# Other places for the transposes of the first and the last experts, for the base rows and for the last additions

## The chip, the cores and the metric

The kernel runs on one core of a Trainium2 chip. The metric is the device time of one execution in microseconds (us). The engines are TensorE (PE, matmuls; PEld its weight loads), VectorE (DVE), ScalarE (ACT), GpSimd (POOL) and SyncE (SP), which issues most DMAs.

## What is computed

One block of a language model, for 512 tokens of width 1024 in fp32: an embedding layer norm, a gated delta-rule branch and a differential-attention branch that are mixed, a layer norm, and then a hierarchical mixture of 16 experts of width 256, two for each token, plus a gated embedding term and the last layer norm. The part that matters here:

```python
def hierarchical_moe(h, w_rg, b_rg, w_re, b_re, w_gate, w_up, w_down):
    ...
    hid = jax.nn.silu(jnp.einsum('bsd,edf->bsef', h, w_gate)) * jnp.einsum('bsd,edf->bsef', h, w_up)
    return jnp.einsum('bsef,efd->bsd', hid * combine[..., None].astype(h.dtype), w_down)
...
    ffn = hierarchical_moe(h, w_router_group[i], b_router_group[i], w_router_expert[i],
                           b_router_expert[i], w_exp_gate[i], w_exp_up[i], w_exp_down[i])
    ple = jax.nn.sigmoid(h @ w_ple_gate[i] + b_ple_gate[i]) * (p[i] @ w_ple_proj[i])
    h = layer_norm(alpha * h + ffn + ple, ln2_g[i], ln2_b[i])
```

## The kernel before

The first 498 us (branches, first norm, router, gated embedding term) are not touched. What follows is the loop over the 16 experts and then `finish`.

Every large product is made of three fp32r matmuls: both operands are split into a high part (a copy on ACT, rounded to fp32r) and a low part (the difference, on DVE). `mm3` issues high by high, high by low and low by high. For weights, `split_to` makes such a split in pieces of [128 x 1024], one ACT copy (L260) and one DVE subtraction (L261) each: sE are the gate and up weights of an expert (four pieces), sD the down weights (two pieces). `load_to` issues the weight loads on SP (L241); a load waits for the landing of the third one before it. `weights` keeps 9 loads and 4 splits ahead of their use.

Expert e goes through these steps:

- `gather` (L1171): an indirect DMA on POOL fetches the rows of up to 128 tokens into xr, one of three buffers, three experts ahead.
- `turn_x` (L1178): 8 transposes on PE (psx) and, for each half, the high part on ACT (L1185) and the low part on DVE (L1187). The result xT is "x(e)" in this text.
- `up` (L1190): 24 matmuls (pup), then the gate: a tanh on ACT (L1194) and two DVE instructions (L1195, L1196); its result is the tile eth.
- `turn_h` (L1199): 2 transposes (psf), a copy on ACT (L1205), the low part on DVE (L1207): hT, "h(e)".
- `down` (L1210): two halves of 6 matmuls (pdn), each scaled into y by ACT (L1220); then an indirect DMA on POOL, the scatter (L1223), writes y to its rows of `planes` in DRAM. `planes` holds two summands for each token. Each scatter waits for the landing of the one before.

The experts are staggered: the list of PE is up(e), x(e+1), down(e-1), h(e). The last two experts, `LAST`, are not scattered. Their scaled results stay in SBUF (`ykeep`, L1217 and L1218), and `finish` adds them by a matmul with a one-hot matrix `to_row`, which POOL makes in 8 instructions (L1288), listed behind the scatter of expert 13.

At e = 13 (IFE) the base rows (`load_base`, acc to the tiles at, 4 loads of 512 KB, L1272) are loaded. Behind the scatter of expert 13 `load_planes` fetches the four planes (pl, 1 MB each, L1277), and `add_planes` adds them to the base rows on DVE (L1283), two additions a tile.

`finish` does the last adding, norm and store for four tiles of 128 tokens: `spread` (PE, plast, L1378), `add_last` (DVE L1385, ACT square sq L1388), `dev` (DVE L1391 and a power on POOL, L204), `norm` (DVE L1395), `turn` (PE transposes into banks pzt, L1404), and `leave`, eight copies with scale and offset for each pair of tiles, on ACT (L1417) or DVE (L1419) as a string of letters says, with two stores on SP (L1422) for each pair.

The program order of each engine is what a scheduler makes of the order in which the instructions are written; PE, DVE and ACT then run their lists strictly in that order. Single PSUM banks come from two pools, `bank` (tag T) and `gbank` (tag G).

Of the kernel before, what the change touches and what calls it, by code (L numbers as in the profile page):

```python
# [19 lines left out]
D = 1024  # L20
NT = 4
# [50 lines left out]
def block_kernel(ctx, tc, x, pT, wA, wB, wO, wM, wPG, wPP, wE, wD, cols, rows, consts, out):  # L72
# [155 lines left out]
    raw, parts = {}, {}  # L228
# [22 lines left out]
    def split_to(n, lo_eng=DVE):  # L251

        while nsplit[0] < min(n, 2 * len(stream)):
            i, j = divmod(nsplit[0], 2)
            k, _, _, shp = stream[i]
            load_to(i + 1)
            n2, w = shp[0] // 2, shp[1]
            r = raw[i][:, j * n2:(j + 1) * n2, :]
            hl = big([2, n2, w], F32R, name="s" + k)
            ACT.activation(hl[:, 0], r, AF.Copy)  # L260
            lo_eng.tensor_tensor(hl[:, 1], r, hl[:, 0].bitcast(F32), op=OP.subtract)  # L261
            parts[i, j] = hl
            if j:
                raw.pop(i)
            nsplit[0] += 1
# [924 lines left out]
    def up(xT, gu, mmul, th=None):  # L1190
        ps = gbank("pup")
        steps(mmul(ps, 8, lambda k: ((xT[:, 0, k, :], xT[:, 1, k, :]), gu(k))))
        th = mid([512], name="eth") if th is None else th
        ACT.activation(th[:, :256], ps[:, :256], AF.Tanh, scale=0.5)  # L1194
        DVE.scalar_tensor_tensor(th[:, :256], th[:, :256], 1.0, ps[:, :256], op0=OP.add, op1=OP.mult)  # L1195
        DVE.tensor_tensor(th[:, 256:], th[:, :256], ps[:, 256:], op=OP.mult)  # L1196
        return th
# [12 lines left out]
    def down(hT, dw, wcol, idxs, mmul, keep=None, y=None):  # L1210
        y = half_slot("y") if keep is None and y is None else y
        for nh in range(2):
            ps = gbank("pdn")
            sl = slice(nh * 512, (nh + 1) * 512)
            steps(mmul(ps, 2, lambda f: ((hT[:, 0, f, :], hT[:, 1, f, :]), dw(f, sl))))
            if keep is not None:
                ACT.activation(keep[:, 0, sl], ps, AF.Copy, scale=wcol)  # L1217
                DVE.scalar_tensor_tensor(keep[:, 1, sl], ps, wcol, keep[:, 0, sl].bitcast(F32), op0=OP.mult, op1=OP.subtract)  # L1218
                continue
            ACT.activation(y[:, sl], ps, AF.Copy, scale=wcol)  # L1220
# [47 lines left out]
    at, pl = [], []  # L1268
# [5 lines left out]
    def load_planes():  # L1274
        pl[:] = [big([2, 1024], name="pl") for _ in range(NT)]
        for t in range(NT):
# [13 lines left out]
    def keep_expert(e):  # L1290
        ykeep[e] = big([2, 1024], F32R, name="ykeep")
        down(hTs.pop(e), weights("D", e), ecol("w", e), None, mm3, keep=ykeep[e])
# [8 lines left out]
    def beyond():  # L1301
        top = nc.values_load(RT["n"][:1, 16:17], min_val=0, max_val=S)
        with tc.If(top > 128):
# [28 lines left out]
            load_planes()  # L1332
            add_planes(*range(NT))
            finish(False)

    for e in range(NE):
        if e + AHEAD < NE:
            rows_of[e + AHEAD] = gather(ecol("s", e + AHEAD), e + AHEAD)
        if e == IFE:
            at = [big([2, 1024], name="at") for _ in range(2)]  # L1340
            load_base()
        if e in LAST:
            find_rows(e)
# [12 lines left out]
        if e + 1 == LAST[0]:  # L1356
            xTs[e + 1] = turn_x(rows_of.pop(e + 1), True)
            finish_expert(e)
            load_planes()
        if e == NE - 1:  # L1360
            with behind(DVE):
                add_planes(1)
# [3 lines left out]
    def finish(add=True):  # L1366
# [57 lines left out]
        with strict(DVE, ACT, PE):  # L1424
# [25 lines left out]
            leave(1, b1, "AVAVAVAV", 2)  # L1450
# [96 lines left out]
```

## Time and profile before

| what | value |
|---|---|
| median of 3 runs | 698.07 us (697.55 to 698.27) |
| the profiled execution | 699.76 us |
| its span, first to last instruction | 698.0 us |
| mean granted TensorE clock | 0.972 |
| TensorE busy | 661.2 us, 95% |
| VectorE busy | 501.3 us, 72% |
| ScalarE busy | 371.8 us, 53% |

The share of an engine is a mean over stages: TensorE is busy for almost the whole span, and the stages in which it isn't are found in the windows and timelines below. A number in brackets in a timeline is the time that the engine stood idle before an instruction, and what it then waited for last. All rows are of one profiled execution, times in us from the start of its span.

### The profile page before, as it was taken

How to read it: one execution, taken by the hardware profiler on the slowest of the kernel's cores; microseconds unless marked ns; L12 is line 12 of the kernel's file. 1: busy time of each engine (PE TensorE's matmuls, PEld its weight loads, DVE VectorE, ACT ScalarE, POOL GpSimd, SP SyncE). 2: the span in 40 equal slices, each digit the busy share in tenths (PEclk: the TensorE clock that was granted, in tenths of full speed). 3: DMA queues.
4: the chain of work that ended last, by engine and by line, in shares of the span. 5: the costliest groups of instructions: out<-in, count | busy, mean ns of one | idle time of the engine just before them, and what ended most of it. 6: DMA issues, size and time to landing. Idle time of an engine off the chain costs nothing. (4 is left out here: it accounts for less than half of the span.)

```text
span 698.0 us, 9556 instructions
## 1 busy us (share of the span) xinstructions
PE 661.2 (95%) x3504; PEld 551.6 (79%) x3505; DVE 501.3 (72%) x921; ACT 371.8 (53%) x695; POOL 98.4 (14%) x110
## 2 busy tenths in 40 slices
PE   8889999999999999999999999999989999997883
PEld 5788888888878878888788888899868888885652
DVE  4864786995358675865525366879689999998593
ACT  6633563472357564754514232134468899978333
POOL 2400030100011212200000010201111222211410
PEclk9899999999999999999999999999989999999995
DMA  8993004213104310312513543575699999994603
GB/s 331 372 418 129 0 13 147 113 61 86 67 1 144 121 62 1 120 61 83 219 61 121 203 161 123 201 297 185 220 375 366 393 361 359 374 360 197 253 0 124
DMA packets 31764, 127.17 MB, mean 182 GB/s; under 512 B 9585, under 2 KB 11249, under 8 KB 20576
## 3 DMA queue, kind: packets, MB, share of 16 engines
q1 hardware_dynamic: 27392, 118.73, 45.8%
q0 software_dynamic: 4320, 7.77, 3.1%
q8 instruction: 29, 0.48, 0.3%
q14 instruction: 23, 0.19, 0.1%
HBM read 111.91 MB, written 22.54 MB: 193 GB/s over the span
## 5 line engine op out<-in xcount | busy, mean ns | idle before, releaser
L283 PE MATMUL pg<-hTh,sA 128*128 128x512 f32 x320 | 129.7, 405 | 0.0
L285 PE MATMUL pg<-hTh,sA 128*128 128x512 f32 x320 | 126.8, 396 | 0.0
L284 PE MATMUL pg<-hTl,sA 128*128 128x512 f32 x320 | 126.7, 396 | 0.0
L261 DVE TENSOR_TENSOR sE<-wE,sE 128x1024 fp32r<-128x1024 f32 x64 | 75.1, 1218 | 0.3 <-ACT sE L260 0.3
L285 PEld LDWEIGHTS pg<-hTh,sA 128*128 128x128 f32 x320 | 60.2, 188 | 13.1
L283 PEld LDWEIGHTS pg<-hTh,sA 128*128 128x128 f32 x320 | 60.3, 188 | 11.6
L284 PEld LDWEIGHTS pg<-hTl,sA 128*128 128x128 f32 x320 | 60.3, 189 | 11.2
L260 ACT ACTIVATE sE<-wE 128x1024 fp32r<-128x1024 f32 x64 | 64.2, 1068 | 0.5 <-PE pg L285 0.4
L260 ACT ACTIVATE sA<-wA 128x1024 fp32r<-128x1024 f32 x40 | 41.4, 1054 | 37.3 <-PE pg L285 25.7
L261 DVE TENSOR_TENSOR sA<-wA,sA 128x1024 fp32r<-128x1024 f32 x40 | 48.5, 1218 | 15.3 <-ACT sA L260 15.3
L283 PE MATMUL pup<-sE,xT 128*128 128x512 f32 x128 | 53.4, 417 | 1.5 <-ACT xT L1185 1.4
L285 PE MATMUL pup<-sE,xT 128*128 128x512 f32 x128 | 52.3, 409 | 2.1 <-DVE xT L1187 2.1
L284 PE MATMUL pup<-sE,xT 128*128 128x512 f32 x128 | 52.1, 407 | 0.0
L261 DVE TENSOR_TENSOR sD<-wD,sD 128x1024 fp32r<-128x1024 f32 x32 | 37.8, 1221 | 4.8 <-ACT sD L260 4.6
L284 PE MATMUL pg<-sPG,H1H 128*128 128x262 f32 (+1 forms) x128 | 36.6, 286 | 0.0
L283 PE MATMUL pg<-sPG,H1H 128*128 128x262 f32 (+1 forms) x128 | 36.5, 286 | 0.0
L285 PE MATMUL pg<-sPG,H1L 128*128 128x262 f32 (+1 forms) x128 | 36.4, 285 | 0.0
L864 ACT ACTIVATE tt<-tt,mn 128x128 f32<-128x128 f32 (+3 forms) x32 | 17.8, 557 | 29.1 <-DVE mn L862 29.0
L260 ACT ACTIVATE sD<-wD 128x1024 fp32r<-128x1024 f32 x32 | 32.4, 1079 | 0.0
L285 PEld LDWEIGHTS pup<-sE,xT 128*128 128x128 f32 x128 | 25.1, 196 | 8.6 <-DVE xT L1187 2.9
L1174 POOL DMA_INDIRECT xr<-h1d,ts x16 | 17.8, 1113 | 98.5 <-PE psx L1183 66.0
L283 PEld LDWEIGHTS pup<-sE,xT 128*128 128x128 f32 x128 | 25.1, 196 | 7.5 <-ACT xT L1185 2.5
(360 smaller groups left out, 1553.1 us busy)
## 6 DMA issues: line engine op xcount, KB each, us to landing
wE<-wE SPq DMA_DIRECT2D x32, 1024.0 KB, 9.3
wA<-wA SPq DMA_DIRECT2D x20, 1024.0 KB, 5.2
wD<-wD SPq DMA_DIRECT2D x16, 1024.0 KB, 10.0
wPG<-wPG SPq DMA_DIRECT2D x4, 1048.0 KB, 8.8
planes<-nil SPq DMA_DIRECT2D x4, 1024.0 KB, 12.4
wO<-wO SPq DMA_DIRECT2D x4, 1024.0 KB, 4.8
wM<-wM SPq DMA_DIRECT2D x4, 1024.0 KB, 4.7
pl<-planes SPq DMA_DIRECT2D x4, 1024.0 KB, 10.9
```

Of the source, the lines that this page charges most:

```text
L260: ACT.activation(hl[:, 0], r, AF.Copy)
L261: lo_eng.tensor_tensor(hl[:, 1], r, hl[:, 0].bitcast(F32), op=OP.subtract)
L283: PE.matmul(ps, lh, rh, start=i == 0, stop=False)
L284: PE.matmul(ps, lh, rl, start=False, stop=False)
L285: PE.matmul(ps, ll, rh, start=False, stop=i == n - 1)
L864: ACT.activation(tt[:, :n], tt[:, :n], AF.Exp, bias=mn[:, m:m + 1], scale=-1.0, accum_out=(s0[:, qt:qt + 1] if m == 0 else s1))
L1174: POOL.indirect_dma_start(out=xr, out_offset=None, in_=h1d, in_offset=bass.IndirectOffsetOnAxis(ap=idx, axis=0), bounds_check=S - 1, oob_i ...
```

## The change

- The transposes of x(1) stand right behind those of x(0), in front of up(0). h(0) is transposed inside up(1), after 15 of its 24 matmuls.
- x(15) is transposed right behind x(14). h(14) is transposed inside up(15), and h(15) inside down(14), between its halves. The gate of 15 is issued behind the last weight split.
- The base rows are loaded behind all weights, right in front of planes 0 and 1; planes 2 and 3 follow when expert 15 is written.
- The additions of plane 0 stand behind up(15), those of plane 1 between down(14) and down(15).
- In `finish` the first pair of tiles takes its four pzt banks from `bank`, the second pair three from `gbank` and one from `bank`; the second pair's copies are "VAVVAVAV" (V is DVE) and not "AVAVAVAV".

The core of the diff:

```diff
-    def up(xT, gu, mmul, th=None):
+    def up(xT, gu, mmul, th=None, inside=None):
         ps = gbank("pup")
-        steps(mmul(ps, 8, lambda k: ((xT[:, 0, k, :], xT[:, 1, k, :]), gu(k))))
+        for k, _ in enumerate(mmul(ps, 8, lambda k: ((xT[:, 0, k, :], xT[:, 1, k, :]), gu(k)))):
+            if k == 4 and inside is not None:
+                inside()
         th = mid([512], name="eth") if th is None else th
+        last = split_at.get((len(stream) - 1, 1))
+        if inside is None or last is None:
+            gate(th, ps)
+        else:
+            with tc.issue_after(last[0]), tc.issue_after(last[1]):
+                gate(th, ps)
+        return th
+
+    def gate(th, ps):
...
+    EARLY = (0, LAST[0])
+    late = {}
+
+    def turn_into(e, th):
+        hTs[e] = turn_h(th, True)
 
     for e in range(NE):
         if e + AHEAD < NE:
             rows_of[e + AHEAD] = gather(ecol("s", e + AHEAD), e + AHEAD)
-        if e == IFE:
-            at = [big([2, 1024], name="at") for _ in range(2)]
-            load_base()
         if e in LAST:
             find_rows(e)
+        if e == 0:
+            xTs[e + 1] = turn_x(rows_of.pop(e + 1), True)
         gus = [weights("E", (e, i), loads=ahead(e), splits=SPLITS) for i in range(2)]
-        th = up(xTs.pop(e), lambda k: gus[k // 4](k % 4), mm3)
+        th = up(xTs.pop(e), lambda k: gus[k // 4](k % 4), mm3, inside=late.pop(e - 1, None))
+        if e + 1 < NE and e + 1 != LAST[0] and e not in EARLY:
+            xTs[e + 1] = turn_x(rows_of.pop(e + 1), True)
+        if e in EARLY or e == NE - 1:
+            late[e] = partial(turn_into, e, th)
         if e == NE - 1:
+            load_planes(2, 3)
             with behind(DVE):
                 add_planes(0)
-        if e + 1 < NE and e + 1 != LAST[0]:
-            xTs[e + 1] = turn_x(rows_of.pop(e + 1), True)
-        if e - 1 in LAST:
-            keep_expert(e - 1)
+            keep_expert(e - 1, inside=late.pop(e))
+            with behind(DVE):
+                add_planes(1)
         elif e and e != LAST[0]:
             finish_expert(e - 1)
-        hTs[e] = turn_h(th, True)
+        if e not in EARLY and e != NE - 1:
+            turn_into(e, th)
         if e + 1 == LAST[0]:
             xTs[e + 1] = turn_x(rows_of.pop(e + 1), True)
             finish_expert(e)
-            load_planes()
-        if e == NE - 1:
-            with behind(DVE):
-                add_planes(1)
+            xTs[e + 2] = turn_x(rows_of.pop(e + 2), True)
+            at = [big([2, 1024], name="at") for _ in range(2)]
+            load_base()
+            load_planes(0, 1)
     keep_expert(NE - 1)
...
                 if t % 2 == 0:
-                    banks.append(gbank("pzt") if i < 3 else bank("pzt"))
+                    banks.append(bank("pzt") if t == 0 or i == 3 else gbank("pzt"))
...
-            leave(1, b1, "AVAVAVAV", 2)
+            leave(1, b1, "VAVVAVAV", 2)
```

The scheduler turns this into other rows on each engine. Three places follow; lines of the changed kernel are a few numbers higher (the split L261 is L262, the DVE copy of x L1187 is L1189, the gate on DVE L1195 is L1208, the tanh L1194 is L1207).

DVE at the start of the loop, before: the last addition in front of the experts (PP), six splits of the weights of experts 0 and 1, the gate of expert 0 (eth), and the copies of x(1) (xT_4650).

```order
L1031 TENSOR_TENSOR PP_3691<-h_485_3131,PP_3691 128x258
L261 TENSOR_TENSOR sE_4604<-wE_3902,sE_4604 128x1024
...
L261 TENSOR_TENSOR sE_4637<-wE_3906,sE_4637 128x1024
L1195 SCALAR_TENSOR_TENSOR eth_4646<-eth_4646,pup_4603 128x256
L1187 TENSOR_TENSOR xT_4650<-psx_4651,xT_4650 128x512
L1196 TENSOR_TENSOR eth_4646<-eth_4646,pup_4603 128x256
L1187 TENSOR_TENSOR xT_4650<-psx_4658,xT_4650 128x512
```

DVE at the same place, after:

```order
L1033 TENSOR_TENSOR PP_3691<-h_485_3131,PP_3691 128x258
L1189 TENSOR_TENSOR xT_4597<-psx_4598,xT_4597 128x512
L1189 TENSOR_TENSOR xT_4597<-psx_4605,xT_4597 128x512
L262 TENSOR_TENSOR sE_4619<-wE_3902,sE_4619 128x1024
...
L262 TENSOR_TENSOR sE_4652<-wE_3906,sE_4652 128x1024
L1208 SCALAR_TENSOR_TENSOR eth_4661<-eth_4661,pup_4618 128x256
L1209 TENSOR_TENSOR eth_4661<-eth_4661,pup_4618 128x256
```

The copies of x(1) have moved from behind the six splits to in front of them.

ACT at expert 13, before: the copy of h(12) (hT), the tanh of expert 13 (eth_5880), the splits of the down weights of 13 (sD) and of the weights of 14 (sE).

```order
L1205 ACTIVATE hT_5832<-psf_5829 128x256
L1194 ACTIVATE eth_5880<-pup_5843 128x256
L260 ACTIVATE sD_5844<-wD_5607 128x1024
L260 ACTIVATE sD_5853<-wD_5607 128x1024
L260 ACTIVATE sE_5862<-wE_5644 128x1024
L260 ACTIVATE sE_5871<-wE_5644 128x1024
L260 ACTIVATE sE_5886<-wE_5646 128x1024
```

ACT at the same place, after (the tanh is eth_5874):

```order
L1217 ACTIVATE hT_5832<-psf_5829 128x256
L261 ACTIVATE sD_5838<-wD_5607 128x1024
L261 ACTIVATE sD_5847<-wD_5607 128x1024
L261 ACTIVATE sE_5856<-wE_5644 128x1024
L261 ACTIVATE sE_5865<-wE_5644 128x1024
L261 ACTIVATE sE_5880<-wE_5646 128x1024
L1207 ACTIVATE eth_5874<-pup_5837 128x256
```

Five of the six splits have moved in front of the tanh.

ACT at the last two experts, before: the tanh of 14, the copy of h(14), the two copies of x(15), the four last splits (sD of experts 14 and 15) and the tanh of 15 (eth_6074).

```order
L1194 ACTIVATE eth_6007<-pup_5982 128x256
L1205 ACTIVATE hT_6029<-psf_6026 128x256
L1185 ACTIVATE xT_6011<-psx_6012 128x512
L1185 ACTIVATE xT_6011<-psx_6019 128x512
L260 ACTIVATE sD_6038<-wD_5801 128x1024
...
L260 ACTIVATE sD_6065<-wD_5841 128x1024
L1194 ACTIVATE eth_6074<-pup_6037 128x256
```

ACT at the same place, after:

```order
L1187 ACTIVATE xT_5963<-psx_5964 128x512
L1187 ACTIVATE xT_5963<-psx_5971 128x512
L1207 ACTIVATE eth_6018<-pup_5993 128x256
L1217 ACTIVATE hT_6055<-psf_6052 128x256
L261 ACTIVATE sD_6028<-wD_5801 128x1024
...
L261 ACTIVATE sD_6061<-wD_5835 128x1024
L1207 ACTIVATE eth_6070<-pup_6027 128x256
```

The copies of x(15) have moved in front of the tanh of 14; the copy of h(14), whose transposes now stand inside up(15), still stands in front of the four splits. DVE has the subtractions in the same order.

## Rows read from the trace of the kernel before

**Rows 1.** Windows: stretch, length; busy PE, PEld, DVE, ACT, POOL; clock, DMA, GB/s.

```profile
508.00:515.30 7.30, 6.04 (x15) 4.76 (x16) 6.68 (x10) 3.35 (x5) 0.00 (x0) 0.53 1.00 396
...
580.00:610.00 30.00, 30.00 (x147) 24.69 (x146) 28.83 (x35) 27.44 (x39) 7.01 (x7) 1.00 0.99 365
...
631.00:637.00 6.00, 4.68 (x29) 4.04 (x30) 5.51 (x7) 6.00 (x8) 0.00 (x0) 1.00 0.76 307
...
641.00:645.00 4.00, 3.44 (x9) 2.44 (x8) 4.00 (x4) 4.00 (x6) 0.00 (x0) 0.57 0.12 47
```

**Rows 2.** Timeline of PE, loop start: start, length, line, operation, count, [idle before].

```profile
498.17 1.25 PE L1183 MATMUL psx<-cst,xr 128*128 128x128 f32 x10
...
509.26 0.80 PE L285 MATMUL pup<-sE,xT 128*128 128x512 f32 x1 [2.05 <-DVE xT L1187]
...
517.40 1.03 PE L1183 MATMUL psx<-cst,xr 128*128 128x128 f32 x8
```

**Rows 3.** Timeline of PE, expert 13 and the step behind it.

```profile
630.54 0.39 PE L285 MATMUL pup<-sE,xT 128*128 128x512 f32 x1
...
632.32 0.44 PE L1202 MATMUL psf<-cst,eth 128*128 128x128 f32 x2 [1.38 <-DVE eth L1196]
...
640.43 0.73 PE L283 MATMUL pdn<-sD,hT 128*128 128x512 f32 x2 [3.12 <-ACT sD L260]
```

**Rows 4.** Timeline of DVE, loop start.

```profile
501.38 6.89 DVE L261 TENSOR_TENSOR sE<-wE,sE 128x1024 fp32r<-128x1024 f32 x6
```

**Rows 5.** Timeline of ACT, expert 13.

```profile
630.97 0.38 ACT L1194 ACTIVATE eth<-pup 128x256 f32<-128x256 f32 x1 [4.64 <-PE pup L285]
```

**Rows 6.** Timeline of DVE, from the last gate to the last copy.

```profile
662.16 0.42 DVE L1195 SCALAR_TENSOR_TENSOR eth<-eth,pup 128x256 f32<-128x256 f32 x1 [2.05 <-ACT eth L1194]
...
678.22 2.48 DVE L1283 TENSOR_TENSOR at<-at,pl 128x1024 f32<-128x1024 f32 x2
...
685.15 0.81 DVE L1395 TENSOR_SCALAR at<-at,st 128x1024 f32<-128x1024 f32 x1 [0.66 <-POOL st L204]
...
689.19 1.91 DVE L1419 TENSOR_SCALAR z<-pzt,col 128x256 f32<-128x256 f32 x4 [2.32 <-ACT z L1417]
```

**Rows 7.** Tile xT: ns of one (min/median/max), first and last start, forms.

```profile
L1187 DVE TENSOR_TENSOR xT<-psx,xT x32: 678/684/693, 499.5 to 654.7; 128x512 fp32r<-128x512 f32 x32
```

**Rows 8.** Tile sD, its copy on ACT.

```profile
L260 ACT ACTIVATE sD<-wD x32: 1048/1084/1095, 507.0 to 657.2; 128x1024 fp32r<-128x1024 f32 x32
```

**Rows 9.** Timeline of SP's DMA queue: base rows, planes, stores.

```profile
622.13 2.94 SPq L1272 DMA_DIRECT2D at<-acc  x4
...
650.71 2.10 SPq L1277 DMA_DIRECT2D pl<-planes  x4
...
686.07 5.39 SPq L1422 DMA_DIRECT2D out<-z  x4
```

**Rows 10.** Timeline of PE, the last transposes.

```profile
685.19 0.69 PE L1404 MATMUL pzt<-cst,at 128*128 128x128 f32 x2 [2.61 <-ACT z L1417]
```

**Rows 11.** Timeline of POOL: an early addition, the last scatters, to_row, a power.

```profile
19.85 6.81 POOL L460 TENSOR_TENSOR x<-x,emb 128x1024 f32<-128x1024 f32 x2 [0.52 <-ACT x L410]
...
638.46 1.62 POOL L1223 DMA_INDIRECT planes<-y,tdi  x1 [8.34 <-ACT hT L1205]
646.89 1.53 POOL L1223 DMA_INDIRECT planes<-y,tdi  x1 [6.80 <-ACT y L1220]
648.47 5.61 POOL L1288 TENSOR_SCALAR to_row<-cst,tf 128x128 fp32r<-128x128 f32 x8
...
678.39 1.46 POOL L204 TENSOR_TENSOR st<-st,half 128x1 f32<-128x1 f32 x1 [1.67 <-DVE st L1391]
```

**Rows 12.** Tile sB, an early weight, its subtraction on DVE.

```profile
L261 DVE TENSOR_TENSOR sB<-wB,sB x4: 1225/1228/3393, 24.4 to 31.2; 128x1040 fp32r<-128x1040 f32 x4
```

**Rows 13.** Tile st, the power on POOL.

```profile
L204 POOL TENSOR_TENSOR st<-st,half x4: 547/560/1459, 676.1 to 684.6; 128x1 f32<-128x1 f32 x4
```

**Rows 14.** Tile planes: landing times of the scatters.

```profile
DMA to landing us min/median/max: 3.8/9.0/12.4
```

More of the change, by code (lines that the diff above doesn't have):

```diff
@@ L1 @@
 import math
+from functools import partial
 from contextlib import ExitStack, contextmanager
@@ L227, in block_kernel @@
     where = {(k, i): n for n, (k, i, _, _) in enumerate(stream)}
-    raw, parts = {}, {}
+    raw, parts, split_at = {}, {}, {}
     nload, nsplit = [0], [0]
@@ L262, in split_to @@
             parts[i, j] = hl
+            split_at[i, j] = nc.cur_bb.bb.instructions[-2:]
             if j:
@@ L1196, in up @@
         DVE.tensor_tensor(th[:, 256:], th[:, :256], ps[:, 256:], op=OP.mult)
-        return th
     def turn_h(th, split, hT=None):
@@ L1208, in turn_h, with down @@
         return hT
-    def down(hT, dw, wcol, idxs, mmul, keep=None, y=None):
+    def down(hT, dw, wcol, idxs, mmul, keep=None, y=None, inside=None):
         y = half_slot("y") if keep is None and y is None else y
@@ L1218, in down @@
                 DVE.scalar_tensor_tensor(keep[:, 1, sl], ps, wcol, keep[:, 0, sl].bitcast(F32), op0=OP.mult, op1=OP.subtract)
+                if nh == 0 and inside is not None:
+                    inside()
                 continue
@@ L1266, in block_kernel @@
     to_row, ykeep = {}, {}
-    at, pl = [], []
+    at, pl = [], {}
     def load_base():
@@ L1272, in load_base, with load_planes @@
             nc.sync.dma_start(at[t // 2][:, t % 2, :], acc[t * 128:(t + 1) * 128, :])
-    def load_planes():
-        pl[:] = [big([2, 1024], name="pl") for _ in range(NT)]
-        for t in range(NT):
+    def load_planes(*tiles):
+        for t in tiles:
+            pl[t] = big([2, 1024], name="pl")
             nc.sync.dma_start(pl[t].rearrange("p c d -> p (c d)"),
@@ L1288, in find_rows, with keep_expert @@
             POOL.tensor_scalar(to_row[e][:, t, :], iota, 128.0 * t, RT["row"][:, e:e + 1], op0=OP.add, op1=OP.is_equal)
-    def keep_expert(e):
+    def keep_expert(e, inside=None):
         ykeep[e] = big([2, 1024], F32R, name="ykeep")
-        down(hTs.pop(e), weights("D", e), ecol("w", e), None, mm3, keep=ykeep[e])
+        down(hTs.pop(e), weights("D", e), ecol("w", e), None, mm3, keep=ykeep[e], inside=inside)
     def mm1(ps, n, term):
@@ L1331, in beyond @@
             load_base()
-            load_planes()
+            load_planes(*range(NT))
             add_planes(*range(NT))
             finish(False)
+    EARLY = (0, LAST[0])
+    late = {}
+    def turn_into(e, th):
+        hTs[e] = turn_h(th, True)
     for e in range(NE):
@@ L1358, in block_kernel @@
             finish_expert(e)
-            load_planes()
-        if e == NE - 1:
-            with behind(DVE):
-                add_planes(1)
+            xTs[e + 2] = turn_x(rows_of.pop(e + 2), True)
+            at = [big([2, 1024], name="at") for _ in range(2)]
+            load_base()
+            load_planes(0, 1)
     keep_expert(NE - 1)
```

## The prediction

> **What bounds the kernel now.** I read the windows by stage first, since the change touches only what follows 498 us. In the middle of the expert loop TensorE is busy 30.00 of 30 us at full clock [rows 1]: nothing but fewer matmuls could shorten it, and the change removes none. 36 matmuls of 512 columns and 10 transposes make one expert. From ten transposes in 1.25 us [rows 2] one costs about 0.11; 147 such instructions in 30 us, 46 to an expert, is one expert per 9.4 us [rows 1], so a 512-column matmul costs (9.4 - 1.1)/36 = 0.231 us. What can be won lies at both ends of the loop and behind it, where TensorE waits and where its granted clock is then 0.53 and 0.57 of full speed, close to the lower of its two levels, 1.2 and 2.4 GHz [rows 1]. The timeline of TensorE names each wait and its releaser [rows 2, 3], and the timelines of VectorE (DVE) and ScalarE (ACT) what stood ahead of the releaser [rows 4, 5]. Since all three run their lists strictly in order, a wait is a question of what is listed in front.
>
> The reader sees three things. At the start TensorE waits 2.05 us for the copy of x(1) on DVE [rows 2], which stands behind six weight splits that take 6.89 us [rows 4]. At expert 13, ACT idles 4.64 us in front of the tanh of expert 13 [rows 5], with all six weight splits listed behind it, and TensorE then waits 1.38 and 3.12 us [rows 3]. At the end DVE begins the last gate at 662.16 and the last norm at 685.15 [rows 6].
>
> **The start: -4.7 us.** x(1) is now transposed straight behind x(0): 16 transposes from 498.17 [rows 2], done by about 500. Its two DVE copies (0.684 each [rows 7], 0.60 from start to start, if their ends overlap by 0.08 as those of the splits do) go ahead of the six splits, so the splits begin at 501.4 + 1.2 = 502.6 and end at 502.6 + 6.89 = 509.5 [rows 4]; one ends every 1.14 us. The first pair lets the second half of expert 0 run (503.8 to 506.5); the next pairs feed expert 1 (about 506.1 and 507.2, 508.4 and 509.5). Expert 1 has 15 matmuls (3.5) behind it at about 510.0; then h(0) is transposed in its middle, which waits for the gate of expert 0 on DVE, behind the sixth split: to 510.3. Two transposes and nine matmuls (2.3) end it at 512.65. The transposes of x(2) come there; before, at 517.40 [rows 2]. So -4.75: 2.05 is the wait, the rest the low clock (0.53 over 7.30 us costs up to 7.30 x 0.47 = 3.4 [rows 1]), less what the splits now hold up. Weights are no bar if they come as before; the DMA queues are 0.99 busy there [rows 1], which is rival 3.
>
> **Expert 13 to the last gate: -7.2 more.** Expert 13's up ended at 630.93 [rows 3]; less 4.75 it is 626.2. Then 12 matmuls of down(12) (2.8), a wait for the gate of 13 that I put at 0.25 (between nothing and the 1.38 of now: five of six splits now stand in front of its tanh on ACT, and end about when up(13) ends), 18 transposes (h(13), x(14), x(15): 2.0), and a wait for the split of the down weights 13, 0.95 by going through DVE's list, between 0 and 3.12 [rows 3]: 632.2. Next 36 matmuls of down(13) and up(14) (8.3): 640.5; 15 of up(15) (3.5): 644.0, where h(14) is transposed. ACT copies it (about 0.4, as the tanh of the same size [rows 5]) and splits the first down weights (1.08 [rows 8]): DVE begins its four splits at 645.7, and with 1.14 each is done at 650.3. The gate of 15 stands right behind them. Before, it began at 662.16 [rows 6]: -11.9 together with the start. The price is that ACT idles some 3.4 us in front of the copy of h(14) and TensorE some 2 us in front of h(15), both inside this sum.
>
> **Behind the loop: -1.6.** From the gate of 15 to the last norm DVE has the same instructions and took 685.15 - 662.16 = 22.99 us; I keep that. From the last norm to the last store's issue: before, 685.15 to 691.1, when the last of four DVE copies is over and the last store goes out [rows 6, 9]; TensorE waited 2.61 us for a bank that ACT had to empty [rows 10]. With banks of the other pool for the second pair that wait goes, and of eight copies DVE takes five, so the end is one norm (0.81) and seven copies of about 0.46 (1.91 for four [rows 6]) and 0.3 for the last one's end: 4.3. 5.98 - 4.3 = 1.6. I take all: nothing is late next, as each DVE copy is behind its own transposes.
>
> **What GpSimd costs: +2.2 (0 to 3.5).** The eight to_row operations (5.61 us, 0.70 each) run right behind the scatter of expert 13, now 648.47 to 654.08, beside a nearly idle DVE [rows 11]. The scatter will be at about 641 to 642.5, so that they run to 648, and DVE begins its four splits at 645.7. The trace shows what comes of that: while GpSimd added two tiles (6.81 us for two [rows 11]) one of four equal DVE splits took 3.393 us and not 1.228 [rows 12]. It shows the reverse, too: one of four equal small GpSimd operations took 1.459, the median being 0.560 [rows 13], and it is the one from 678.39 [rows 11], inside DVE's two adds from 678.22 [rows 6]. So either may wait. Some 3.2 of eight operations are left at 645.7: 3.2 x 0.70 = 2.2 us, which I take, as the split is the nearer row; 5 left give 3.5, and nothing if DVE wins each time. (The Trainium skill, "SBUF — State Buffer", section "Who interferes with whom", says that a DVE instruction with two SBUF inputs and a GpSimd instruction that reads SBUF exclude each other for the whole instruction of whichever began first; the stretched split agrees. Taking turns by that rule, four splits would each wait for one operation, 4 x 0.70 = 2.8, and the time would be 687.6.)
>
> **Base rows and planes: +0.3 (0 to 2).** The base rows (4 issues, 2.94 us of SP's time at 622.13) go behind the last weights, in front of the planes [rows 9]. Each scatter waits for its predecessor's landing, 9.0 us at the median and 3.8 for one in a free queue [rows 14]: those of experts 12 and 13 come at about 635 and 641 instead of 638.46 and 646.89 [rows 11]. The last lands at about 645 and planes 0 and 1 are issued behind it, before at 650.71 [rows 9]. One plane is 1 MB, at the 365 GB/s of the loop [rows 1] 2.9 us and about 1.7 to begin: landed at 649.6. The first add wants it at 650.3 + 0.8 = 651.1. The 1.5 us are a thin cover; 2 MB of base rows (5.7 us at 365 GB/s) lie between the scatters, hence 0.3 and up to 2.
>
> **Sum.** -11.9 - 1.6 + 2.2 + 0.3 = -11.0. The profiled execution took 699.76 with a span of 698.0; the median of the runs is 698.07, so I set the sum against the median, which is the span within 0.1: **687.0 us**.
>
> **The rivals.**
> 1. *GpSimd yields.* The small operations of [rows 13] waited, not DVE. Then the 2.2 goes: 684.8, and 683.6 if both waits at expert 13 also vanish (0.25 + 0.95).
> 2. *The clock falls again.* Between 626 and 646 TensorE still stops two or three times, and runs 18 transposes. A stop of 3.12 us was followed by a granted clock of 0.57 over 4 us [rows 1, 3]: 4 x 0.43 = 1.7 us lost. Once or twice more: 688.7 to 690.4. For: the waits stay, only shorter; against: the wait of 1.38 us lies in a stretch that was granted in full, 631 to 637 [rows 1], and none that I expect is longer than 2.
> 3. *The transfers take the start back.* The queues are 0.99 busy in the loop [rows 1]; if the weights are what sets the period, the 4.7 is waited out in the loop: 691.7. Against: TensorE is busy 30.00 of 30 there, so weights wait for it and not it for them.
> 4. *The order at the end brings nothing.* If a split of 13 or of 14 just waits where the gate waited, only start and tail are left: 698.07 - 4.75 - 1.6 = 691.7. Against: the ACT idle time in front of the tanh had all six splits behind it [rows 5], and they need nothing from TensorE but buffers.
> 5. *Slower: the planes come late.* The base rows, four transfers in a row, are put between the last scatters and the planes. If scatters 11, 12 and 13 each took the longest landing of the trace, 12.4 instead of 9.0, 9.0 and 3.8 [rows 14], the planes would come 15.4 later, 13.9 beyond their cover: 687.0 + 13.9 = 700.9. It decides from planes landing behind 662, 11 us late. Against: the median is 9.0 while the weights keep the queues 0.99 busy [rows 1], and they are over by then.
>
> **How the numbers follow.** Forecast 687.0 (685.7 to 688.6) 0.45; rival 1 0.22; rival 2 0.20; rival 3 0.05; rival 4 0.04; rival 5 0.03; 3 and 4 together, 1.6 us faster than now or less, 0.01. The range takes in the forecast, nearly all of rivals 1 and 2, and the bounds of GpSimd (3.5) and of the base rows (2) together, 687.0 + 1.3 + 1.7 = 690.0, and reaches to the first hundredths of rivals 3 and 4: 683.6 to 691.5. About 0.15 is left out. A measurement of this kernel tells 0.2% (1.4 us) from no change; each of the first five cases is more than 6 us faster: faster 0.96, within 0.2% 0.02 (rivals 3 and 4 together, and rival 5 with planes that land just behind 662), slower 0.02 (rival 5 in full).
>
> **What would show each step.** The transposes of x(2) at 512.6 and no wait for x(1); DVE's first split behind two copies. No ACT idle in front of the tanh of 13. The last gate at 650 to 653 on DVE, with four splits of 1.14 or stretched to 1.9 (then GpSimd's share). The first add right behind the gate, or waiting for a plane. The last norm 23.0 us behind the gate, the last store 4.3 us behind that. It is wrong if the gate comes later than 655, or a wait for a plane of more than 2 us stands at the first add.

## The result and the profile after

The changed kernel takes 688.04 us (median of 4 runs, 687.27 to 690.28), the kernel before, run beside it, 698.17 us (697.55 to 701.93): a ratio of 0.9849, 95% interval 0.9807 to 0.9891. The forecast was 687.0 in a range of 683.6 to 691.5. The profiled execution took 687.71 us, its span is 685.9. Taken of 698.17 us, the interval stands for 7.6 to 13.5 us won. Two of the four times of the experiment e1 (821.84 and 2277.81 us) fell into a slow state and are left out below.

The rows of after show the steps in the order of the prediction. Lines of the changed kernel are a few numbers higher. Each row is start, length, engine, line, operation, output <- input, count and, in brackets, the idle time before it and what ended that.

TensorE at the start of the loop:

```profile
497.83 1.91 PE L1185 MATMUL psx<-cst,xr 128*128 128x128 f32 x16
...
503.50 0.50 PE L286 MATMUL pup<-sE,xT 128*128 128x512 f32 x1 [0.75 <-DVE sE L262]
...
510.06 0.41 PE L1214 MATMUL psf<-cst,eth 128*128 128x128 f32 x2 [0.26 <-DVE eth L1209]
...
512.39 1.03 PE L1185 MATMUL psx<-cst,xr 128*128 128x128 f32 x8
```

Before, TensorE waited 2.05 us here [rows 2], and ahead of that once more:

```profile
506.48 0.50 PE L283 MATMUL pup<-sE,xT 128*128 128x512 f32 x1 [0.49 <-ACT xT L1185]
```

Both waits are gone; 0.75 for the delayed split and 0.26 for the gate of expert 0 have come. The transposes of x(2) come at 512.39; 512.65 was foreseen.

Now experts 13 to 15, TensorE, then ACT, then DVE:

```profile
628.97 0.44 PE L1214 MATMUL psf<-cst,eth 128*128 128x128 f32 x2
629.25 1.91 PE L1185 MATMUL psx<-cst,xr 128*128 128x128 f32 x16
631.97 0.73 PE L285 MATMUL pdn<-sD,hT 128*128 128x512 f32 x2 [0.81 <-ACT sD L261]
...
643.92 0.38 PE L1214 MATMUL psf<-cst,eth 128*128 128x128 f32 x2
...
651.52 0.44 PE L1214 MATMUL psf<-cst,eth 128*128 128x128 f32 x2 [1.69 <-DVE eth L1209]
```

```profile
623.27 2.97 ACT L261 ACTIVATE sE<-wE 128x1024 fp32r<-128x1024 f32 x3
626.11 0.40 ACT L1207 ACTIVATE eth<-pup 128x256 f32<-128x256 f32 x1
...
644.34 0.38 ACT L1217 ACTIVATE hT<-psf 128x256 fp32r<-128x256 f32 x1 [3.33 <-PE psf L1214]
```

```profile
644.76 0.42 DVE L1219 TENSOR_TENSOR hT<-psf,hT 128x256 fp32r<-128x256 f32 x1 [2.84 <-ACT hT L1217]
645.70 4.97 DVE L262 TENSOR_TENSOR sD<-wD,sD 128x1024 fp32r<-128x1024 f32 x4 [0.52 <-ACT sD L261]
650.60 0.41 DVE L1208 SCALAR_TENSOR_TENSOR eth<-eth,pup 128x256 f32<-128x256 f32 x1
651.04 0.42 DVE L1209 TENSOR_TENSOR eth<-eth,pup 128x256 f32<-128x256 f32 x1
651.38 1.22 DVE L1297 TENSOR_TENSOR at<-at,pl 128x1024 f32<-128x1024 f32 x1
```

ACT's idle time of 4.64 us in front of the tanh of 13 [rows 5] is gone, and of TensorE's waits of 1.38 and 3.12 us [rows 3] 0.81 is left. DVE begins its last splits at 645.70 (645.7 was foreseen), but they take 4.97 us, not 4.6. The gate of 15 is at 650.60, before at 662.16 [rows 6], and the first addition follows without a wait for plane 0. The last norm and copies on DVE:

```profile
674.35 0.82 DVE L1420 TENSOR_SCALAR at<-at,st 128x1024 f32<-128x1024 f32 x1 [0.66 <-POOL st L205]
675.08 2.49 DVE L1444 TENSOR_SCALAR z<-pzt,col 128x256 f32<-128x256 f32 x5
677.75 1.00 DVE L1444 TENSOR_SCALAR z<-pzt,col 128x256 f32<-128x256 f32 x2 [0.18 <-ACT z L1442]
```

The last copy ends 4.4 us behind the start of the last norm, before 5.95 [rows 6]. TensorE's last transposes wait for DVE alone, and no longer 2.61 us for ACT [rows 10]:

```profile
671.29 5.74 PE L1429 MATMUL pzt<-cst,at 128*128 128x128 f32 x26 [2.91 <-DVE st L1410]
```

For comparing traces there is a trap: the first 498 us are the same program in all kernels here, yet the loop's first transposes begin anywhere from 496.87 to 499.42 in fourteen traces. So in this table all times are counted from those transposes (us); the experiments follow below. The times of the rows above need the same care: the changed kernel's loop began at 497.83 and that of the kernel before at 498.17, so a time that agrees in the two scales is 0.34 us later by this count.

| kernel | x(2) transposed | gate of 15 | last norm | last copy ends |
|---|---|---|---|---|
| before | 19.23 | 163.99 | 186.98 | 192.93 |
| before, second trace | 17.92 | 161.93 | 184.92 | 190.86 |
| start alone (e1) | 14.55 | 159.61 | 182.60 | 188.54 |
| changed, start undone (e5) | 16.52 | 154.12 | 177.82 | 182.22 |
| changed | 14.56 | 152.77 | 176.52 | 180.92 |
| changed, second trace (e0) | 14.55 | 152.56 | 175.74 | 180.00 |
| to_row early (e2) | 14.55 | 152.42 | 175.57 | 179.86 |
| to_row twice (e3) | 14.56 | 152.53 | 175.77 | 180.03 |
| base rows back (e4) | 14.56 | 155.16 | 178.48 | 182.88 |
| last copies as before (e6) | 14.55 | 152.47 | 175.64 | 181.59 |
| splits ahead of h(14) (e7) | 14.55 | 149.11 | 174.45 | 178.85 |
| e7 and half of the base rows later (e10) | 14.55 | 149.22 | 172.91 | 177.17 |

By the two profiled executions the change is worth 699.76 - 687.71 = 12.05 us, by the medians 10.1; the interval of 7.6 to 13.5 us takes in both.

### The profile page after: what moved, and what is told of

The parts are those of the page before. It is cut to its first block, busy times and chain, and to the rows that moved or that the text cites. A ratio compares the mean times of both kernels' runs of the same rounds, so it can differ in the third digit from the quotient of the medians.

```text
span 685.9 us, 9547 instructions
## 1 busy us (share of the span) xinstructions
PE 656.9 (96%) x3504; PEld 549.4 (80%) x3505; DVE 501.4 (73%) x922; ACT 371.4 (54%) x694; POOL 101.3 (15%) x110
## 4 chain that ended last, share of the span: by engine, by line
PE 82%; DVE 8%; ACT 4%; DMA 3%; issue 1%; POOL 1%; SPq 0%; ACTq 0%; POOLq 0%; DVEq 0%
PE pg L286 17%; PE pg L287 17%; PE pg L285 17%; PE pup L287 4%; PE pup L285 4%; PE pup L286 4%; PE pdn L285 2%; PE pdn L286 2%; PE pdn L287 2%; DMA wA<-wA 2%; PE psx L1185 2%; PE pov L891 1%; DMA wPP<-wPP 1%; PE psh L370 1%; DVE at L1297 1%
## 5 line engine op out<-in xcount | busy, mean ns | idle before, releaser
L262 DVE TENSOR_TENSOR sE<-wE,sE 128x1024 fp32r<-128x1024 f32 x64 | 75.3, 1219 | 0.3 <-ACT sE L261 0.3
L261 ACT ACTIVATE sE<-wE 128x1024 fp32r<-128x1024 f32 x64 | 64.4, 1069 | 0.5 <-PE pg L287 0.4
L261 ACT ACTIVATE sA<-wA 128x1024 fp32r<-128x1024 f32 x40 | 41.4, 1054 | 35.8 <-PE pg L287 25.4
L262 DVE TENSOR_TENSOR sA<-wA,sA 128x1024 fp32r<-128x1024 f32 x40 | 48.5, 1219 | 13.9 <-ACT sA L261 13.9
L285 PE MATMUL pup<-sE,xT 128*128 128x512 f32 x128 | 51.6, 403 | 0.0
L286 PE MATMUL pup<-sE,xT 128*128 128x512 f32 x128 | 50.4, 394 | 0.7 <-DVE sE L262 0.7
L287 PE MATMUL pup<-sE,xT 128*128 128x512 f32 x128 | 50.4, 394 | 0.0
L262 DVE TENSOR_TENSOR sD<-wD,sD 128x1024 fp32r<-128x1024 f32 x32 | 38.0, 1232 | 4.0 <-ACT sD L261 3.7
L261 ACT ACTIVATE sD<-wD 128x1024 fp32r<-128x1024 f32 x32 | 32.3, 1078 | 0.0
L509 DVE SCALAR_TENSOR_TENSOR acc<-pad,col,acc 128x512 f32<-128x512 f32 x36 | 26.8, 744 | 4.8 <-ACT acc L507 4.6
L286 PEld LDWEIGHTS pup<-sE,xT 128*128 128x128 f32 x128 | 24.1, 188 | 6.1 <-DVE sE L262 1.2
## 6 DMA issues: line engine op xcount, KB each, us to landing
wD<-wD SPq DMA_DIRECT2D x16, 1024.0 KB, 10.1
pl<-planes SPq DMA_DIRECT2D x4, 1024.0 KB, 11.2
```

Source lines behind the costliest of these rows:

```text
L285: PE.matmul(ps, lh, rh, start=i == 0, stop=False)
L286: PE.matmul(ps, lh, rl, start=False, stop=False)
L287: PE.matmul(ps, ll, rh, start=False, stop=i == n - 1)
L509: DVE.scalar_tensor_tensor(acc, pad[:, j:j + 512], w[j], acc, op0=OP.mult, op1=OP.add)
```

## The experiments

**e1_start_only and e5_no_start: what the start is worth.** The first puts the new start into the kernel before, the second takes the same lines out of the changed one. The core of e1:

```diff
+        if e == 0:
+            xTs[e + 1] = turn_x(rows_of.pop(e + 1), True)
...
-        if e + 1 < NE and e + 1 != LAST[0]:
+        if e and e + 1 < NE and e + 1 != LAST[0]:
-        hTs[e] = turn_h(th, True)
+        if e == 0:
+            late[e] = lambda th=th: turn_into(0, th)
+        else:
+            turn_into(e, th)
```

> The kernel before with the start of the change alone: x(1) is transposed right behind x(0), h(0) inside up(1). Theory: the transposes of x(2) come at 512.4 to 512.7 instead of 517.4, nothing of it is lost in the loop, and the time is 4.7 us below that of the kernel before (693.4). Rival: the weights cannot come earlier, the loop waits the gain out, and less than 2 us are left (696 or more). ACT's idle time in front of the tanh of expert 13 (4.64 us) stays in either case.

> The changed kernel with the start as before: x(1) behind up(0), h(0) behind it. Theory (the parts add up): the transposes of x(2) come 19.2 us behind the first ones of the loop, the gate of 15 4.6 us later than in the changed kernel, 157.4 behind them, and the time is 4.4 to 4.7 us above the changed kernel's. Rival: with the later start the planes and scatters have more time, or the loop catches up with its weights, and 2 us or more of the difference are lost by the gate of 15.

e1 took 694.31 and 696.65 us, beside a median of 700.86 (697.84 to 701.55) for the kernel before: 4.2 to 6.6 us less, too few times for an interval, so that here the trace decides. In its trace x(2) is transposed 4.68 us earlier than in the first trace of before, and the gate of 15 is 4.38 and the last copy 4.39 earlier: the loop gives 0.3 of it back, not more. In all eleven traces that have the new start x(2) comes at 14.55 or 14.56 us. ACT's idle time in front of the tanh of 13 is still there (4.59).

e5 took 690.76 us (688.96 to 693.90). Its ratio to the kernel before, 0.9922, stands beside 0.9849 and 0.9876 for the changed kernel, a difference of 3.2 to 5.1 us. In the trace the expectation failed: x(2) came at 16.52, not at 19.2, and the gate of 15 only 1.4 to 1.6 us later than in the two traces of the changed kernel. The waits were those of before, to the hundredth:

```profile
506.10 0.50 PE L285 MATMUL pup<-sE,xT 128*128 128x512 f32 x1 [0.49 <-ACT xT L1187]
...
508.88 0.50 PE L287 MATMUL pup<-sE,xT 128*128 128x512 f32 x1 [2.05 <-DVE xT L1189]
...
514.32 1.04 PE L1185 MATMUL psx<-cst,xr 128*128 128x128 f32 x8
```

The difference is the clock behind them. The windows of 508 to 515.3 us (length; busy and count of PE, PEld, DVE, ACT, POOL; granted clock, DMA share, GB/s), first e5:

```profile
508.00:515.30 7.30, 6.42 (x33) 5.35 (x34) 7.08 (x10) 3.94 (x6) 0.00 (x0) 1.00 1.01 386
```

then the second trace of the kernel before:

```profile
508.00:515.30 7.30, 7.03 (x26) 5.62 (x27) 6.20 (x8) 3.23 (x4) 0.00 (x0) 0.77 1.02 402
```

In the first trace of before it was 0.53 [rows 1]. 1.00 is the level of 2.4 GHz throughout, 0.53 nearly all of the stretch at 1.2 GHz, 0.77 about half of it at either. The same wait was followed by a granted clock of 1.00, 0.77 and 0.53 in three executions. So of the 4.67 us won at the start 16.52 - 14.56 = 1.96 are the waits, which all three executions have, and up to 2.71 are the low clock behind them, which two of them have.

**e11_before_again: the kernel before once more.**

> The kernel before once more, for a second trace. Theory: the waits are the same in each execution (0.49 and 2.05 us for the copies of x(1), 1.38 and 3.14 us at expert 13), while the fall of the granted clock behind them is not; where it doesn't fall at the start, the transposes of x(2) come 16.5 us behind the first ones of the loop (as in e5_no_start), and where it does, 19.2. The time goes with that, 696 to 701. Rival: the fall at the start belongs to the kernel before, and x(2) comes at 19.2 in this trace too, with its granted clock near 0.53 in the 7 us behind the wait.

The waits were the same (0.49, 2.04, 1.38 and 3.11 us); x(2) came at 17.92, between the two values expected, since the clock fell for a part of the stretch only. The gate came 2.06 us earlier than in the first trace, the last copy 2.07. 0.98 us more of the difference between the two spans of 698.0 and 695.0 lie ahead of the loop. The times of the kernel before ran from 695.6 to 702.0 over all the comparisons, and here, compared with itself, it gave a ratio of 1.0025 (1.0001 to 1.0049): a difference of a quarter of a per cent, 1.7 us, is not told by such times. The profiled execution on which the sum was built, at 699.76, lay in the upper part of this spread, the median 1.6 us below it.

**e4_base_back: the base rows back at expert 13.**

```diff
+        if e == IFE:
+            at = [big([2, 1024], name="at") for _ in range(2)]
+            load_base()
...
-            at = [big([2, 1024], name="at") for _ in range(2)]
-            load_base()
             load_planes(0, 1)
```

> The changed kernel with the base rows back at expert 13, ahead of the last weight load. Theory, from the order that the scheduler then builds (the tanh of 13 stands in front of all splits again): the two tiles of the base rows take buffers that the splits of expert 13 want, ACT idles 4 to 5 us in front of that tanh again, TensorE waits for splits of the down weights of 13 as before, and the time is 4 to 6 us above the changed kernel (about 693). Rival, as in the prediction: the base rows are only a matter of transfers between scatters and planes, and the time is that of the changed kernel or 0.3 less (687.7 to 688).

690.82 us (688.77 to 691.72), where e2 and e3, which ran beside it, took 687.40 and 687.24: 3.5 us more, not the 4 to 6 expected. The changed kernel itself did not run beside them; the ratio of e4, 0.9868 (0.9838 to 0.9898), overlaps with both of its ratios, so the traces decide. TensorE and ACT wait as in the kernel before:

```profile
626.42 0.44 PE L1214 MATMUL psf<-cst,eth 128*128 128x128 f32 x2 [1.38 <-DVE eth L1209]
634.54 0.73 PE L285 MATMUL pdn<-sD,hT 128*128 128x512 f32 x2 [3.14 <-ACT sD L261]
636.05 0.50 PE L286 MATMUL pdn<-sD,hT 128*128 128x512 f32 x1 [0.55 <-DVE sD L262]
```

```profile
625.07 0.38 ACT L1207 ACTIVATE eth<-pup 128x256 f32<-128x256 f32 x1 [4.59 <-PE pup L287]
```

So the place of the base rows, which the prediction took for a matter of transfers, changes the order of the splits at expert 13; whether their move alone, without the other edits, would do it was not tried. The gate of 15 comes 2.4 to 2.6 us later than in the two traces of the changed kernel, less than those waits. The likely reason is that the scheduler here also put three of the last four splits in front of the copy of h(14), an order that e7 tries by itself (3.4 to 3.7 us at the gate):

```profile
645.94 2.95 ACT L261 ACTIVATE sD<-wD 128x1024 fp32r<-128x1024 f32 x3
649.32 0.39 ACT L1217 ACTIVATE hT<-psf 128x256 fp32r<-128x256 f32 x1 [0.44 <-PE psf L1214]
```

Why the scheduler orders the splits by the place of the base rows is not shown. That the two tiles take buffers from the splits, as the expectation has it, is a guess: no run moves the tiles and the loads apart.

**e2_rows_early and e3_rows_twice: does GpSimd hold DVE up?** The first makes to_row six experts earlier, the second makes it twice.

```diff
-        to_row[e] = big([4, 128], F32R, name="to_row")
+        to_row[e] = mid([4, 128], F32R, name="to_row")
...
-        if e in LAST:
-            find_rows(e)
+        if e in (8, 9):
+            find_rows(e + 6)
```

```diff
-        for t in range(NT):
+        for t in [*range(NT), *range(NT)]:
             POOL.tensor_scalar(to_row[e][:, t, :], iota, 128.0 * t, RT["row"][:, e:e + 1], op0=OP.add, op1=OP.is_equal)
```

> The changed kernel with the eight to_row operations of GpSimd made in experts 8 and 9, in small tiles of another pool, so that none of them runs beside the last four splits. Theory (GpSimd yields to DVE, with a small remainder): the four splits take 4.63 us and not 4.97, the last gate comes 0.3 us earlier, and the time falls by 0.3 at most, which a time cannot tell. Rival (either may wait, and the changed kernel had luck with the starts): the time falls by 1 us or more.

> The changed kernel with each to_row operation done twice (16 in place of 8), so that GpSimd is busy from 641.5 through all four last splits and the last gate. Theory (GpSimd yields): the 16 operations take 11.2 us plus what they wait, some 14 to 16 us; DVE's four splits take 5.0 to 5.4 us, and the time rises by less than 0.7. Rival (taking turns): each split and each add behind it waits for one operation of 0.70, the splits take 7 us or more and the time rises by 2 to 4 us.

Both take about the time of the changed kernel: 687.40 (685.71 to 689.03) and 687.24 (686.55 to 689.39). Their ratios, 0.9810 (0.9774 to 0.9846) and 0.9818 (0.9784 to 0.9853), overlap with its first, 0.9849; they lie below its second, 0.9876, but the kernel before beside them took 700.86, beside that one 697.17. In the traces the gate of 15 comes at 152.42 and 152.53, in the changed kernel at 152.77 and 152.56. The four last splits, in e2 without GpSimd beside them, then in e3:

```profile
647.25 4.63 DVE L262 TENSOR_TENSOR sD<-wD,sD 128x1024 fp32r<-128x1024 f32 x4 [0.52 <-ACT sD L261]
```

```profile
646.27 4.79 DVE L262 TENSOR_TENSOR sD<-wD,sD 128x1024 fp32r<-128x1024 f32 x4 [0.52 <-ACT sD L261]
```

and GpSimd, in the changed kernel and in e3:

```profile
641.48 7.33 POOL L1302 TENSOR_SCALAR to_row<-cst,tf 128x128 fp32r<-128x128 f32 x8
```

```profile
642.55 18.85 POOL L1302 TENSOR_SCALAR to_row<-cst,tf 128x128 fp32r<-128x128 f32 x16
```

The sixteen operations take 18.85 us where 2 x 5.61 = 11.2 would do, more than the 14 to 16 expected; DVE's four splits lose 0.16 us (0.34 in the first trace of the changed kernel), less than the 0.4 to 0.8 expected. GpSimd does nearly all the waiting. In the changed kernel its longest to_row took 2.417 us, the median 0.708, so it stood out the whole second split. DVE's losses there are 0.27 us on the first split (1.477 for some 1.21), which began within 0.01 us of an operation of 0.709, and 0.09 on the third.

In the changed kernel this is a mild test, since six of the eight operations were over when the splits began. In e7, further below, all eight run beside DVE's splits and what follows them. They take 9.04 us, and three splits take 3.59, where they take 3.50 without them (e9):

```profile
643.09 3.59 DVE L262 TENSOR_TENSOR sD<-wD,sD 128x1024 fp32r<-128x1024 f32 x3
```

```profile
643.79 9.04 POOL L1302 TENSOR_SCALAR to_row<-cst,tf 128x128 fp32r<-128x128 f32 x8
```

The Trainium skill, "SBUF — State Buffer", "Who interferes with whom", says that the one that issues first has the shared ports for its whole instruction and the other is blocked. That GpSimd's operations are held for whole splits agrees with this. That DVE would lose the whole operation it meets does not show: it lost 0.27 us against one of 0.709. Taking turns, as the prediction priced that rule, does not show either.

**e0_after_again and e6_tail_back: the stretch behind the loop.** e6 sets the banks and the string of the last copies back.

```diff
-                    banks.append(bank("pzt") if t == 0 or i == 3 else gbank("pzt"))
+                    banks.append(gbank("pzt") if i < 3 else bank("pzt"))
...
-            leave(1, b1, "VAVVAVAV", 2)
+            leave(1, b1, "AVAVAVAV", 2)
```

> The changed kernel once more, beside the others of this call, for their times on one chip and for a second trace of it. Theory: from the first transposes of the loop to the gate of 15 it takes 152.8 us as in its first trace, and 21.9 (the last addition of a plane and all behind it included, 23.1 to 23.8) from there to the last norm, 23.1 to 23.3 if the granted clock does not fall behind the wait for the gate, 23.8 if it does. Rival: the stretch from the gate to the last norm is always 23.8, whatever the clock.

> The changed kernel with the banks and the string of letters of the last copies as before. Theory: TensorE waits 2.6 us for a bank that ACT empties, the last copy ends 5.9 to 6.0 us behind the start of the last norm and not 4.4, and the time is 1.5 us above that of the changed kernel of this call. Rival: the last store's landing, 4.9 us in the changed kernel and 2.8 before, takes the gain back, and the time is within 0.5.

e0: 687.96 us (686.33 to 688.61). From the gate to the last norm it took 23.18 us, in the first trace 23.75. TensorE waits for the gate of 15 in both, 1.69 us in the first trace (above) and here

```profile
650.84 0.44 PE L1214 MATMUL psf<-cst,eth 128*128 128x128 f32 x2 [1.77 <-DVE eth L1209]
```

and the granted clock behind that differs. The windows from 650 to 655 us, first trace and second:

```profile
650.00:655.00 5.00, 3.23 (x9) 1.73 (x10) 4.97 (x8) 1.05 (x3) 0.00 (x0) 0.77 1.02 429
```

```profile
650.00:655.00 5.00, 3.27 (x12) 1.91 (x13) 4.97 (x8) 0.38 (x1) 0.00 (x0) 1.00 0.86 362
```

In the first, DVE then waits 0.81 us for the last copies of down(14), in the second 0.23. The other traces with this wait (1.61 to 1.69 us) go the same two ways: over the 6 us from the gate on, the clock is 0.72 in the first trace and in e5, which take 23.75 and 23.70 us to the norm, and 1.00 in e0, e2, e3 and e6, which take 23.15 to 23.24. The row of e5:

```profile
651.92:657.92 6.00, 4.84 (x14) 3.11 (x15) 5.88 (x9) 0.51 (x3) 0.57 (x1) 0.72 0.88 371
```

The fall costs 0.6 us here.

e6: 688.67 us (687.61 to 690.47), 0.7 above e0. The last copy ends 5.95 us behind the start of the last norm, 4.26 in e0: the 1.7 us of the trace are near the 1.5 expected, and TensorE waits for ACT again, 1.74 us and not 2.6. At the end of the span 1.29 us of it are left; the last stores land in 3.1 us here and in 4.9 in e0, which is the rival's way of taking a part back. The intervals of the two ratios (0.9859 to 0.9893 and 0.9871 to 0.9912) overlap, so how much reaches the time is open between 0 and 1.7.

**e7_splits_first, e9_splits_rows and e10_base_halves, e12_halves_rows: what is late next.** e7 uses the 3.3 us in which ACT waits for h(14):

```diff
     def turn_into(e, th):
-        hTs[e] = turn_h(th, True)
+        if e == LAST[0]:
+            a, d = split_at[where["D", NE - 1], 0]
+            with tc.issue_after(a), tc.issue_after(d):
+                hTs[e] = turn_h(th, True)
+        else:
+            hTs[e] = turn_h(th, True)
```

> The changed kernel with three of the last four weight splits in front of the copy of h(14) on ACT and DVE, where both stand idle for about 3 us. Theory: DVE splits behind the gate of 14, the gate of 15 comes when up(15) ends, 149.2 us behind the first transposes of the loop and not 152.8, TensorE doesn't wait for it, and the time falls by 3 to 3.6. Rival: plane 0, issued 3.3 us ahead of that, has not landed, DVE waits 1 to 3 us for it in front of the first addition, and the time falls by 0.5 to 2.5.

> As e7_splits_first, and the to_row operations of GpSimd made in experts 8 and 9. Theory (GpSimd yields): 0.3 us less than e7_splits_first or the same. Rival: with the splits right behind the scatter, all eight operations run beside them, and the time falls by 1 us or more against e7_splits_first.

e7 took 686.61 (686.11 to 687.40), 1.35 below e0; the intervals of the two ratios (0.9837 to 0.9872 and 0.9859 to 0.9893) overlap. The gate came at 149.11 us (149.2 expected), but then plane 0 was late, as the rival had it:

```profile
648.07 0.41 DVE L1208 SCALAR_TENSOR_TENSOR eth<-eth,pup 128x256 f32<-128x256 f32 x1
648.51 0.42 DVE L1209 TENSOR_TENSOR eth<-eth,pup 128x256 f32<-128x256 f32 x1
650.90 1.35 DVE L1297 TENSOR_TENSOR at<-at,pl 128x1024 f32<-128x1024 f32 x1 [1.97 <-DMA pl<-planes]
```

The planes were issued from 646.10 on SP, so plane 0 lands some 4.8 us behind its issue; the prediction had estimated 4.6. e9, with to_row early as well, took 686.93 (684.99 to 688.55), the same as e7 within its spread: the gate came at 149.00, but the planes were issued 1.3 us later and the wait for plane 0 was 3.45 us. Why they came later is open.

The transfers in front of plane 0 are the chain of scatters and 2 MB of base rows, of which the additions of planes 0 and 1 need one half. e10 is e7 with the other half behind planes 0 and 1:

```diff
-            load_base()
+            load_base(0, 1)
             load_planes(0, 1)
...
+            load_base(2, 3)
             load_planes(2, 3)
```

> As e7_splits_first, with the base rows of tiles 2 and 3 (1 MB) loaded behind planes 0 and 1. Theory: the scatter of 12 shares the queues with 1 MB and not 2 MB, lands 1.5 to 2.5 us earlier, and so do the scatter of 13 and plane 0; DVE's wait of 2.0 us for plane 0 falls to 0.5 or less, and the time is 1.5 to 2 us below that of e7_splits_first against the kernel before (ratio 0.983 instead of 0.9855). Rival: the scatters land no earlier (they wait for the weights or for their own chain), the wait stays at 1.5 us or more, and the ratio stays at 0.985.

> As e10_base_halves, and the to_row operations of GpSimd made in experts 8 and 9. Theory: the first three of the last splits take 3.50 us and not 3.71, the gate of 15 and the end come 0.2 to 0.3 us earlier, which the times cannot tell (685.0, ratio 0.982 to 0.983). Rival: the operations in experts 8 and 9 hold up gathers or scatters of the loop, and plane 0 is issued later than in e10_base_halves, by 1 us or more, as it was in e9_splits_rows against e7_splits_first.

e10 took 685.26 us (683.74 to 686.15), a ratio of 0.9827 to the kernel before (0.981 to 0.9844), and DVE adds without a wait:

```profile
648.72 0.42 DVE L1209 TENSOR_TENSOR eth<-eth,pup 128x256 f32<-128x256 f32 x1
649.05 1.30 DVE L1297 TENSOR_TENSOR at<-at,pl 128x1024 f32<-128x1024 f32 x1
```

Planes 0 and 1 were issued 144.1 us behind the loop's first transposes, in e7 147.1. e12 took 685.65 (683.17 to 687.97), ratio 0.9821 (0.9795 to 0.9847): the same within what can be measured, with its first three splits at 3.50 us and planes no later than in e10. At the last copy both beat the changed kernel by 3.7 us in its first trace and by 2.8 in its second; by the ratios (0.9827 and 0.9821 beside the changed kernel's 0.9849 and 0.9876) it is 1.5 to 3.8 us of time. The intervals overlap with that of the first, 0.9849, and lie below that of the second.

## Why the prediction was right, step by step

**Start, -4.75.** -4.67 in the two profiled executions, and the single times came as worked out: counted from the loop's first transposes, the splits begin at 4.40 for 4.43 and x(2) comes at 14.56 for 14.48. (The 0.99 for the DMA queues "there" is that of 580 to 610 us; the row of the start has 1.00, which changes nothing.) What the step booked as one price is two: 1.96 us for the waits, in each trace that has them, and up to 2.71 for the low clock, which is a matter of the execution (e5, e11). Against e11's trace, whose clock fell less, the same new start is worth 17.92 - 14.56 = 3.4.

**Expert 13 to the last gate, -7.2.** From x(2) to the gate of 15: 144.76 us before, 138.21 after, so -6.55, or -6.9 without GpSimd's 0.34. The wait for the gate of 13 put at 0.25 is too short to be listed, that for the split put at 0.95 is 0.81. Counted from the loop's first transposes, h(14) is transposed at 146.09 (145.8 foreseen) and the splits begin at 147.87 (147.5): the agreement of 643.92 and 645.70 with 644.0 and 645.7 is 0.3 us too good, since this loop began 0.34 earlier. The order was read rightly from the lists. What the prediction didn't ask is which edit makes that order: e4 shows that without the move of the base rows the waits at expert 13 come back. That move was booked at +0.3 as a transfer.

**GpSimd, +2.2.** The mis-sized term: 0.34 us. One part is the count: the scatter came at 640.47, ahead of the 641 to 642.5 foreseen, so that two of the eight operations were left at 645.70 and not 3.2, worth 1.4 by the prediction's own rule. The step that failed is the choice between the two rows: the stretched split [rows 12] had met an addition of several us that was already running, the stretched power [rows 13] had met two additions of DVE that followed each other. The second is nearer to the case at hand, a queue of DVE splits, and e3 and e7, with more operations beside the splits, show that rival 1 was right in its mechanism.

**Base rows, +0.3.** No wait at the first addition, so 0, and the cover was thin as told: e7 needed plane 0 three us earlier and had to wait 1.97. The 1.7 us to begin, for which the working shows no row, is what 16 KB loads took to land in the trace of before (X<-XBd, the median).

**Behind the loop, -1.6.** From the norm to the end of the last copy 5.95 to 4.40, so -1.55 (4.26 in e0, -1.7); the 5.98 of the prediction is 5.95 by its own rows, too. The 22.99 us from gate to norm, which the sum kept, became 23.75, +0.76, and 23.18 where the clock didn't fall. The fall is rival 2's mechanism at another place: between 626 and 646 us, where that rival had it, the granted clock was 1.00; it fell behind the wait for the gate of 15, and cost 0.6 and not 1.7.

**The sum.** In the two traces: -4.67 - 6.55 + 0.76 - 1.55 = -12.0 at the last copy, where -11.0 was foreseen. GpSimd cost 1.9 us less than was put down, the base rows 0.3 less, the stretch from the gate to the norm 0.8 more, and experts 13 to 15 gave 0.3 less. The median fell by 10.1, in an interval of 7.6 to 13.5, so the times cannot tell 11 from 12, and that 688.04 lies only 1.0 above the forecast is in part luck. The sum is a difference of two single executions and was set against a median that lay 1.6 us below the one it was read from. That this median equals the span of that execution within 0.1 is a coincidence: span and time of one execution are 1.8 us apart (698.0 and 699.76). What the 1.6 us are is not shown piece by piece. The times go with the mean granted clock: over the comparisons of the experiments, executions of the kernel before with 0.976 took 695.6 to 697.9, those with 0.969 to 0.972 took 698.5 to 702.0, and the profiled one had 0.972. So a part of what the change removed in that trace, the low clock at the start above all, is in some executions of the kernel before and not in others. Errors of 1 to 2 us went against each other. Of the other rivals, 3 fell with e1 (0.3 of 4.7 given back), 4 with the order and the trace, 5 with the first addition.

## What to carry to other kernels

In kernels whose engines run fixed lists, look for the wait in what stands ahead of the releaser, and ask of each edit, a moved load too, whether it changes the order that the scheduler builds. When a stretch is won, find the next arrival and its slack before pricing the next gain: here plane 0 was next, and of the 3.4 to 3.7 us that e7 won at the gate in the traces only 1.2 to 2.1 reached the last copy, and with half of the base rows moved behind planes 0 and 1 it was 2.8 to 3.7. Price a wait of TensorE by its length, and what the granted clock does behind it as a range from nothing to what a trace shows, for two traces of one kernel can differ by that. And compare times of two traces only from a mark that both have.

## What the runs showed of the hardware that was not expected

The granted clock behind one and the same wait of 2.05 us was 0.53, 0.77 and 1.00 in three executions (7.3 us from 508 on), and behind waits of 1.61 to 1.77 us it was 0.72 in two executions and 1.00 in four (6 us from the gate on). GpSimd beside an unbroken row of DVE instructions, most of them with two inputs in SBUF, did nearly all the waiting: 16 operations of 0.70 us took 18.85, at a cost of 0.16 us to DVE's four splits, and in e7 eight took 9.04, at a cost of 0.09 to three. And the same program before the loop took 496.87 to 499.42 us in fourteen traces, so that only times counted from a common mark tell differences below 2 us.
